# Seven-product calls of a second FFN: two sums of weight blocks move from the vector engine to accumulating transfers, and one product moves to the end

## The chip, the core and the metric

One core of a Trainium2 chip runs the whole kernel. The metric is the device time in microseconds of one execution. The kernel before was run three times: 1250.19, 1249.74 and 1250.16 us, median 1250.16 us.

Engines carry the profile's names: PE (TensorE, matrix products), PEld (its weight loads), DVE (VectorE), ACT (ScalarE), POOL (GpSimd) and SP (SyncE). SP only issues transfers; POOL issues the accumulating ones and otherwise does a little arithmetic. Each engine takes its instructions in order.

## What is computed

The reference is one decoder layer over 512 tokens of width 1024, followed by a normalisation. What matters here is its last feed-forward step:

```python
x = x + 0.5 * swiglu_ffn(rmsnorm(x, ffn2_norm), ffn2_w_in, ffn2_w_down)

def swiglu_ffn(x, w_in, w_down):
    a, b = jnp.split(x @ w_in, 2, axis=-1)
    return (jax.nn.silu(a) * b) @ w_down
```

`ffn2_w_in` is 1024 x 5632 (twice 2816 columns, for `a` and for `b`), `ffn2_w_down` is 2816 x 1024. All is fp32.

## The kernel before

**Products in three parts.** To keep fp32 accuracy, each operand is split into a rounded high part and a low rest. `split` (L118 to L126) makes `wh` from a weight tile on ACT (L124) and then `wl` as the difference on DVE (L125). The tags `wh` and `wl` have three buffers each. Every block then costs three matrix instructions: high x high, high x low rest of the activations, low rest x high.

**The seven-product calls.** The second FFN works on columns of `w_in` in steps of two 128-column tiles, `f` = 0, 2, ..., 20. The first three steps (0, 2, 4) are plain. The eight from `f` = 6 to `f` = 20 are done by `fast_in` (L1141 to L1209), a scheme with seven half-size products in place of eight; a call is named here by its `f` (call 6, call 8, ...). With the four blocks of the call's weights named a11 and a12 (columns of `a`, upper and lower half of the rows) and their counterparts in the `b` columns, a call does this:

- `s1` = upper plus lower half of the `b` columns: SP loads the one (L1150), POOL then issues an accumulating transfer from DRAM that adds the other (L1151).
- `ra` (tile `wraw`, two buffers, shared with the loads of `w_down`) holds a11 and a12.
- `s3` likewise from a load (L1154) and an accumulating transfer (L1155); `q22` is a plain load (L1157).
- `s2` = `s1` + a11 (DVE, L1184) and `s4` = `s2` + a12 (DVE, L1192), each in a buffer of its own. `s1`, `s3`, `q22`, `s2` and `s4` share the tag `wq` with five buffers.
- the products, in source order: `s1` x t1, a11 x b11, a12 x b21, `s2` x t2, `s4` x b22, `s3` x t3, `q22` x t4. A product is named by its activations: t1, b11, b21, t2, b22, t3, t4. In PE's rows t1h and t1l are the parts of t1, while b21 and b22 read the tiles uh and ul. Each product has 24 instructions of 128 x 256: 12 for the first of two output tiles (j = 0), 12 for the second.
- between them, copies and additions out of PSUM (ACT at L1186, L1189, L1195; DVE at L1199, L1201), and at the end tanh, two multiplications and the split into `gh` and `gl` (L1206 to L1209). t2, t3 and t4 go on accumulating in the same PSUM half, so t3 waits for the copy at L1195 and t4 for the addition at L1201.

**Around the calls.** The `f` go in groups of six, six, six and four. After the first call of a group `down2` (L1211) does the previous group's product with `w_down`, 144 (for the last group 96) instructions of 128 x 512. So calls 8, 10 and 12 stand back to back, then comes a `down2`, then 14, 16 and 18, another `down2`, call 20, and the last `down2` with the final normalisation.

**Order.** A scheduler sets the order of the instructions on each engine, and the pools decide which buffer a tile gets and so what a load waits for. Within a call's source order the scheduler may interleave products.

Of the kernel before, what the change touches and what calls it, by code (L numbers as in the profile page):

```python
# [15 lines left out]
ALU = mybir.AluOpType  # L16
# [68 lines left out]
def kernel(ctx, tc, x, mem, ffn1_norm, ffn1_w_in, ffn1_w_down, mix_norm, w_in, a_re, a_im, log_dt,  # L85
                             b_re, b_im, c_re, c_im, d_skip, w_glu, rel_table, w_up_attn, mem_norm, w_kv, w_up_mem,
                             w_out, ffn2_norm, ffn2_w_in, ffn2_w_down, final_norm, onehot, parity, out):
    nc = tc.nc
    V, S, G, TE = nc.vector, nc.scalar, nc.gpsimd, nc.tensor
    x, mem, out = x[0], mem[0], out[0]  # L90

    def sb_pool(name, side="left"):
        return tc.tile_pool(name=name, bufs=1, side=side, reuse_waits="tile")
# [13 lines left out]
    def load_chunk(w, k0, nk, c0, ncol):  # L107
        raw = wpool.tile([P, nk, ncol], F32, name="wraw", tag="wraw", bufs=2)
        nc.sync.dma_start(raw, w[k0 * P:(k0 + nk) * P, c0:c0 + ncol].rearrange("(k p) c -> p k c", p=P))
        return raw  # L110
# [9 lines left out]
    def split(raw, eng=V):  # L120
        _, nk, n = raw.shape
        h = wpool.tile([P, nk, n], F32R, name="wh", tag="wh", bufs=3)
        l = wpool.tile([P, nk, n], F32R, name="wl", tag="wl", bufs=3)
        S.activation(h, raw, AF.Copy)  # L124
        eng.tensor_tensor(l, raw, h.bitcast(F32), op=ALU.subtract)  # L125
        return h, l  # L126
# [15 lines left out]
    def split_plain(src, h, l, eng=V):  # L142
        S.activation(h, src, AF.Copy)  # L143
        eng.tensor_tensor(l, src, h.bitcast(F32), op=ALU.subtract)
# [26 lines left out]
    def ps_tile(tag, bufs=None):  # L171
        return ps["pool"].tile([P, T], F32, name="ps_" + tag, tag="ps_" + tag, bufs=ps["mm"] if tag == "mm" else bufs)
# [845 lines left out]
    with sb_pool("att") as ap:  # L1018
# [9 lines left out]
        for hp in range(2):  # L1028
            pacc = ps_tile("acc", 1)
            for r in range(4):  # L1030
# [12 lines left out]
                j = d % 2  # L1043
# [16 lines left out]
    op = wo_stack.enter_context(sb_pool("wo", "right"))  # L1060
# [34 lines left out]
    left, right = slice(0, HT), slice(HT, T)  # L1095
# [45 lines left out]
    def fast_in(w, f, pool, g):  # L1141

        def quarter(nm):
            return pool.tile([P, 4, 2 * P], F32, name=nm, tag="wq", bufs=5)

        def src(k0, c0):
            return w[0][k0 * P:(k0 + 4) * P, c0 + f * P:c0 + (f + 2) * P].rearrange("(k p) c -> p k c", p=P)

        s1 = quarter("s1")
        nc.sync.dma_start(s1, src(0, FF))  # L1150
        nc.gpsimd.dma_start(s1, src(4, FF), accum_op=ALU.add)  # L1151
        ra = load_chunk(w[0], 0, KD, f * P, 2 * P)
        s3 = quarter("s3")
        nc.sync.dma_start(s3, src(0, FF))  # L1154
        nc.gpsimd.dma_start(s3, src(0, 0), accum_op=ALU.add)  # L1155
        q22 = quarter("q22")
        nc.sync.dma_start(q22, src(4, FF))  # L1157
        a11, a12 = ra[:, :4, :], ra[:, 4:, :]
        px = [ps_tile("mm") for _ in range(2)]
        py = [ps_tile("mm") for _ in range(2)]  # L1160
        a = [pool.tile([P, T], F32, name="ff_a", tag="ff_a", bufs=3) for _ in range(2)]
        e5 = [pool.tile([P, HT], F32, name="ff_e", tag="ff_e", bufs=2) for _ in range(2)]

        def moving(n):
            if n in comb[0]:
                return [(comb[0][n][:, k], comb[1][n][:, k]) for k in range(4)]
            base, half = {"b21": (4, left), "b22": (4, right)}[n]
            return [(uh[base + k][:, half], ul[base + k][:, half]) for k in range(4)]

        def product(block, n, dst, half, start):  # L1170
            h, l = split(block)
            rhs = moving(n)
            for j in range(2):
                o, cols = dst[j][:, half], slice(j * P, (j + 1) * P)
                for k in range(4):
                    st = dict(start=start and k == 0, skip_group_check=True)
                    TE.matmul(o, h[:, k, cols], rhs[k][0], stop=False, **st)  # L1177
                    st["start"] = False
                    TE.matmul(o, h[:, k, cols], rhs[k][1], stop=False, **st)  # L1179
                    TE.matmul(o, l[:, k, cols], rhs[k][0], stop=k == 3, **st)  # L1180

        product(s1, "t1", py, right, True)
        s2 = quarter("s2")
        V.tensor_tensor(s2, s1, a11, op=ALU.add)  # L1184
        for j in range(2):
            S.activation(e5[j], py[j][:, right], AF.Copy)  # L1186
        product(a11, "b11", px, left, True)
        for j in range(2):
            S.activation(a[j][:, left], px[j][:, left], AF.Copy)  # L1189
        product(a12, "b21", py, left, False)  # L1190
        s4 = quarter("s4")
        V.tensor_tensor(s4, s2, a12, op=ALU.add)  # L1192
        product(s2, "t2", px, left, False)
        for j in range(2):
            S.activation(a[j][:, right], px[j][:, left], AF.Copy)  # L1195
        product(s4, "b22", py, right, False)
        product(s3, "t3", px, left, False)
        for j in range(2):
            V.tensor_tensor(a[j], a[j], py[j], op=ALU.add)  # L1199
        for j in range(2):  # L1200
            V.tensor_tensor(px[j][:, right], px[j][:, left], e5[j], op=ALU.add)  # L1201
        product(q22, "t4", px, left, False)

        for j in range(2):
            t = pool.tile([P, T], F32, name="ff_t", tag="ff_t", bufs=2)
            S.activation(t, a[j], AF.Tanh, scale=-0.5)  # L1206
            V.scalar_tensor_tensor(t, t, 1.0, a[j], op0=ALU.subtract, op1=ALU.mult)
            V.tensor_tensor(t, t, px[j], op=ALU.mult)
            split_plain(t, *g[f + j])  # L1209
# [79 lines left out]
    for f0, nf in groups:  # L1289
        for f in range(f0, f0 + nf, 2):  # L1290
            g.update(hidden(fp, f, 2))
            if f < 6:
                ffn_in(ffn2_w_in, f, fp, g, True, 3, steps2)
            else:
                fast_in(ffn2_w_in, f, fp, g)
                if f == 6:
                    natural_x2()
            if f == f0 and pend is not None:
                down2(*pend, False)
        pend = (f0, nf)  # L1300
# [34 lines left out]
```

## Time and profile before

The profiled execution took 1250.94 us; its span, from the first to the last instruction, is 1249.2 us. So 1.7 us lie around the span, and this execution is 0.8 us over the median of the runs.

| What | Value |
|---|---|
| Median of three runs | 1250.16 us |
| Profiled execution / its span | 1250.94 / 1249.2 us |
| Mean granted TensorE clock | 0.998 |
| Busy: PE / DVE / ACT / POOL | 1231.3 / 793.7 / 466.8 / 101.6 us |
| Seven-product calls, first and last rows of L1177 | 953.4 to 1222.7 us |

How to read it: the page gives busy time per engine and the chain of work that ended last. The timelines give single instructions as start, duration, engine, line, operation and tiles, with the idle time before it and what ended that in brackets. "DMA to landing" counts from the issue of a transfer to the arrival of its data.

### The profile page before, as it was taken

Reading aid. Unit: us, or ns where it says so; the run is one execution under the profiler, and the core shown is the slowest. Engines: PE = TensorE matmul, PEld = TensorE weight load, DVE = VectorE, ACT = ScalarE, POOL = GpSimd, SP = SyncE. Lnnn points to the kernel's source line nnn. Section 1 sums busy time; section 2 is a strip of 40 time slices with the busy share of each in tenths; the row PEclk is TensorE's granted clock in tenths of the full one; section 3 lists DMA queues with packets and bytes.
Section 4 is the critical chain, followed back from the end, with each engine's and each line's share of the span. In section 5 each row is a group of like instructions: output and inputs, shape, how many; then the busy total and the mean of one; then the engine's idle time right before and its main releaser. Section 6 shows DMA issues by size and latency. Waiting matters only on the chain.

```text
span 1249.2 us, 17053 instructions
## 1 busy us (share of the span) xinstructions
PE 1231.3 (99%) x6692; PEld 1046.2 (84%) x6692; DVE 793.7 (64%) x1514; ACT 466.8 (37%) x731; POOL 101.6 (8%) x83
## 2 busy tenths in 40 slices
PE   8999999999999999999999999999999999999997
PEld 6888888788888889998877788888789899899896
DVE  7999556875637666754536654554498557657664
ACT  4332232224325443224433544343345445345343
POOL 3000000000003023230000000002100001001002
PEclk9999999999999999999999999999999999999999
DMA  6233423764317755644118221335625457457411
GB/s 194 93 117 115 140 93 85 180 188 143 107 51 248 239 172 156 203 143 126 52 34 194 68 68 43 101 111 164 172 82 157 115 148 183 123 148 182 122 61 67
DMA packets 165767, 162.01 MB, mean 130 GB/s; under 512 B 28180, under 2 KB 149076, under 8 KB 165396
## 3 DMA queue, kind: packets, MB, share of 16 engines
q1 hardware_dynamic: 133488, 137.68, 35.3%
q0 software_dynamic: 8576, 8.65, 4.7%
q10 hardware_dynamic: 23624, 14.61, 4.0%
q8 instruction: 52, 0.85, 0.3%
q14 instruction: 27, 0.22, 0.1%
HBM read 145.94 MB, written 16.16 MB: 130 GB/s over the span
## 4 chain that ended last, share of the span: by engine, by line
PE 94%; DMA 2%; DVE 2%; ACT 1%; issue 0%; SPq 0%; ACTq 0%; DVEq 0%
PE ps_mm L133 20%; PE ps_mm L134 20%; PE ps_mm L135 20%; PE ps_mm L1179 4%; PE ps_mm L1180 4%; PE ps_mm L1177 4%; PE ps_mm L1235 3%; PE ps_mm L1237 3%; PE ps_mm L1236 3%; PE ps_acc L905 1%; PE ps_sc L898 1%; PE ps_sc L742 1%; DMA wraw<-in_ffn_w_in_dram 1%; DMA wraw<-in_xattn_w_kv_dram 1%; DVE wl L125 1%; PE ps_mm L833 1%
## 5 line engine op out<-in xcount | busy, mean ns | idle before, releaser
L124 ACT ACTIVATE wh<-wraw 128x1024 fp32r<-128x1024 f32 (+2 forms) x226 | 211.2, 938 | 468.4 <-PE ps_mm L134 321.2
L125 DVE TENSOR_TENSOR wl<-wraw,wh 128x1024 fp32r<-128x1024 f32 (+2 forms) x226 | 248.6, 1102 | 145.8 <-ACT wh L124 139.8
L133 PE MATMUL ps_mm<-uh,wh 128*128 128x512 f32 x736 | 288.9, 393 | 1.2 <-ACT wh L124 0.9
L135 PE MATMUL ps_mm<-uh,wl 128*128 128x512 f32 x736 | 287.9, 391 | 0.0
L134 PE MATMUL ps_mm<-ul,wh 128*128 128x512 f32 x736 | 287.6, 391 | 0.0
L133 PEld LDWEIGHTS ps_mm<-uh,wh 128*128 128x128 f32 x736 | 138.3, 188 | 30.1 <-issue 1.7
L135 PEld LDWEIGHTS ps_mm<-uh,wl 128*128 128x128 f32 x736 | 138.2, 188 | 28.7 <-issue 0.2
L134 PEld LDWEIGHTS ps_mm<-ul,wh 128*128 128x128 f32 x736 | 138.3, 188 | 28.5 <-issue 0.2
L217 POOL TENSOR_TENSOR sqacc<-sqacc,sqk 128x512 f32<-128x512 f32 x12 | 20.2, 1681 | 680.7 <-ACT sqk L216 680.6
L134 PE MATMUL ps_mm<-gl,wh 128*128 128x512 f32 x176 | 70.0, 398 | 0.0
L133 PE MATMUL ps_mm<-gh,wh 128*128 128x512 f32 x176 | 69.9, 399 | 0.0
L135 PE MATMUL ps_mm<-gh,wl 128*128 128x512 f32 x176 | 69.8, 398 | 0.0
L1236 PE MATMUL ps_mm<-wl,gh 128*128 128x512 f32 x176 | 69.4, 394 | 0.0
L1237 PE MATMUL ps_mm<-wh,gl 128*128 128x512 f32 x176 | 69.1, 394 | 0.0
L1235 PE MATMUL ps_mm<-wh,gh 128*128 128x512 f32 x176 | 67.6, 395 | 0.0
L125 DVE TENSOR_TENSOR wl<-s,wh 128x1024 fp32r<-128x1024 f32 x32 | 39.2, 1224 | 42.6 <-ACT wh L124 42.5
L124 ACT ACTIVATE wh<-s 128x1024 fp32r<-128x1024 f32 x32 | 33.9, 1061 | 61.4 <-PE ps_mm L1237 26.1
L143 ACT ACTIVATE gh<-ff_t 128x512 fp32r<-128x512 f32 x44 | 27.1, 627 | 52.3 <-DVE ff_t L315 33.3
L135 PEld LDWEIGHTS ps_mm<-gh,wl 128*128 128x128 f32 x176 | 33.0, 188 | 8.2 <-issue 0.2
L133 PEld LDWEIGHTS ps_mm<-gh,wh 128*128 128x128 f32 x176 | 33.0, 188 | 8.2 <-issue 0.2
L1237 PEld LDWEIGHTS ps_mm<-wh,gl 128*128 128x128 f32 x176 | 33.1, 188 | 7.7
L1236 PEld LDWEIGHTS ps_mm<-wl,gh 128*128 128x128 f32 x176 | 33.2, 188 | 7.5
(415 smaller groups left out, 2444.1 us busy)
## 6 DMA issues: line engine op xcount, KB each, us to landing
wraw<-in_ffn_w_in_dram SPq DMA_DIRECT2D x34, 1024.0 KB, 5.1
wraw<-in_w_in_dram SPq DMA_DIRECT2D x25, 1024.0 KB, 5.3
wraw<-in_ffn_w_down_dram SPq DMA_DIRECT2D x12, 768.0 KB, 4.6
s<-in_ffn_w_in_dram SPq DMA_DIRECT2D x16, 512.0 KB, 3.6
s<-in_ffn_w_in_dram POOLq DMA_DIRECT2D x16, 512.0 KB, 6.2
wraw<-in_ffn_w_down_dram SPq DMA_DIRECT2D x8, 1024.0 KB, 5.1
wraw<-in_ffn_w_down_dram SPq DMA_DIRECT2D x10, 512.0 KB, 3.5
wraw<-in_xattn_w_kv_dram SPq DMA_DIRECT2D x4, 1024.0 KB, 8.1
```

What stands on the lines that cost most here:

```text
L124: S.activation(h, raw, AF.Copy)
L125: eng.tensor_tensor(l, raw, h.bitcast(F32), op=ALU.subtract)
L133: TE.matmul(ps, h[:, k, :], rhs[k][0], start=first and k == 0, stop=False)
L134: TE.matmul(ps, h[:, k, :], rhs[k][1], start=False, stop=False)
L135: TE.matmul(ps, l[:, k, :], rhs[k][0], start=False, stop=last and k == n - 1)
L143: S.activation(h, src, AF.Copy)
L1177: TE.matmul(o, h[:, k, cols], rhs[k][0], stop=False, **st)
L1179: TE.matmul(o, h[:, k, cols], rhs[k][1], stop=False, **st)
L1180: TE.matmul(o, l[:, k, cols], rhs[k][0], stop=k == 3, **st)
L1235: TE.matmul(pd[r], gh[:, tok], h, start=st, stop=False)
L1236: TE.matmul(pd[r], gh[:, tok], l, start=False, stop=False)
L1237: TE.matmul(pd[r], gl[:, tok], h, start=False, stop=en)
```

## The change

The two DVE additions go. In their place POOL issues accumulating transfers from one place of SBUF to another: `s1` += a11 after the first product's split, and `s1` += a12 after the split for t2. The tiles `s2` and `s4` no longer exist; the fourth block sum's product, b22, stands last in source order, and the addition of `py` into `a` follows it.

```diff
         product(s1, "t1", py, right, True)
-        s2 = quarter("s2")
-        V.tensor_tensor(s2, s1, a11, op=ALU.add)
+        nc.gpsimd.dma_start(s1, a11, accum_op=ALU.add)
...
         product(a12, "b21", py, left, False)
-        s4 = quarter("s4")
-        V.tensor_tensor(s4, s2, a12, op=ALU.add)
-        product(s2, "t2", px, left, False)
+        product(s1, "t2", px, left, False)
+        nc.gpsimd.dma_start(s1, a12, accum_op=ALU.add)
         for j in range(2):
             S.activation(a[j][:, right], px[j][:, left], AF.Copy)
-        product(s4, "b22", py, right, False)
         product(s3, "t3", px, left, False)
-        for j in range(2):
-            V.tensor_tensor(a[j], a[j], py[j], op=ALU.add)
         for j in range(2):
             V.tensor_tensor(px[j][:, right], px[j][:, left], e5[j], op=ALU.add)
         product(q22, "t4", px, left, False)
+        product(s1, "b22", py, right, False)
+        for j in range(2):
+            V.tensor_tensor(a[j], a[j], py[j], op=ALU.add)
```

From here on acc1 is the transfer `s1` += a11 (L1183 of the changed kernel) and acc2 is `s1` += a12 (L1191). Lines from L1185 on are one or two lower in the changed kernel than before.

POOL's order from call 8 on. `s1_` and `s3_` are the sums of a call. Before, `s1_8914` belongs to call 8, `s1_9158` to call 10, `s1_9402` to call 12, `s1_9838` to call 14:

```order
L1151 DMA s1_8914<-in_ffn2_w_in_dram 128x4x256
L1155 DMA s3_8919<-in_ffn2_w_in_dram 128x4x256
L1151 DMA s1_9158<-in_ffn2_w_in_dram 128x4x256
L1155 DMA s3_9163<-in_ffn2_w_in_dram 128x4x256
L1151 DMA s1_9402<-in_ffn2_w_in_dram 128x4x256
L1155 DMA s3_9407<-in_ffn2_w_in_dram 128x4x256
```

In the changed kernel `s1_8912` is of call 8, `s1_9154` of call 10, `s1_9396` of call 12 and `s1_9830` of call 14; `wraw_` is the call's `ra`:

```order
L1183 DMA s1_8912<-wraw_8915 128x1024
L1191 DMA s1_8912<-wraw_8915 128x1024
L1151 DMA s1_9396<-in_ffn2_w_in_dram 128x4x256
L1183 DMA s1_9154<-wraw_9157 128x1024
L1155 DMA s3_9401<-in_ffn2_w_in_dram 128x4x256
L1191 DMA s1_9154<-wraw_9157 128x1024
L1151 DMA s1_9830<-in_ffn2_w_in_dram 128x4x256
L1183 DMA s1_9396<-wraw_9399 128x1024
```

Four transfers a call pass through POOL instead of two, and the next-but-one sum of a later call (`s1_9396` of call 12) stands ahead of call 10's acc1.

SP's order at the same place, before (`wraw_9405` is call 12's):

```order
L109 DMA wraw_9161<-in_ffn2_w_in_dram 128x8x256
L1150 DMA s1_9158<-in_ffn2_w_in_dram 128x4x256
L109 DMA wraw_9405<-in_ffn2_w_in_dram 128x8x256
L1154 DMA s3_9163<-in_ffn2_w_in_dram 128x4x256
L1157 DMA q22_9166<-in_ffn2_w_in_dram 128x4x256
L1150 DMA s1_9402<-in_ffn2_w_in_dram 128x4x256
```

And in the changed kernel (`wraw_9399` is call 12's, `q22_9162` call 10's):

```order
L109 DMA wraw_9157<-in_ffn2_w_in_dram 128x8x256
L1157 DMA q22_9162<-in_ffn2_w_in_dram 128x4x256
L109 DMA wraw_9399<-in_ffn2_w_in_dram 128x8x256
L1150 DMA s1_9396<-in_ffn2_w_in_dram 128x4x256
L1154 DMA s3_9401<-in_ffn2_w_in_dram 128x4x256
L1157 DMA q22_9404<-in_ffn2_w_in_dram 128x4x256
L109 DMA wraw_9638<-in_ffn2_w_down_dram 128x4x512
```

Call 12's `wraw_9399` takes call 8's buffer, which acc1 and acc2 of call 8 now read, so its load waits until both have landed; the load of `s1_9396` has moved right behind it on SP.

PE's order in call 10 of the changed kernel, at the end of the first half of t3 (output tile `ps_mm_9164`); the rows with `uh4` and `ul4` are the first of b22, whose `wh_9350` is made from `s1` after acc2:

```order
L1180 MATMUL ps_mm_9164<-t3h_7861,wl_9293 128x256
L1177 MATMUL ps_mm_9166<-uh4_101,wh_9350 128x256
L1179 MATMUL ps_mm_9166<-ul4_109,wh_9350 128x256
L1177 MATMUL ps_mm_9167<-uh4_101,wh_9350 128x256
L1179 MATMUL ps_mm_9167<-ul4_109,wh_9350 128x256
L1177 MATMUL ps_mm_9165<-t3h_7861,wh_9292 128x256
```

Although b22 is last in the source, the scheduler has put four of its 24 rows between the halves of t3; after the other half of t3 follow 16 more, then all of t4, then the last four and t1 of the next call. Before, all 24 rows of b22 stood between t2 and t3.

## Prediction

> **What bounds the kernel now.** I read the page first: busy time and the chain that ended last.
>
> ```profile
> PE 1231.3 (99%) x6692; PEld 1046.2 (84%) x6692; DVE 793.7 (64%) x1514; ACT 466.8 (37%) x731; POOL 101.6 (8%) x83
> PE 94%; DMA 2%; DVE 2%; ACT 1%; issue 0%; SPq 0%; ACTq 0%; DVEq 0%
> ```
>
> An average says little about one stage, so next the windows around the calls 8 to 12, 14 to 18, the last call and the end (columns: window, length, then busy time of PE, PEld, DVE, ACT, POOL, clock, DMA share, GB/s).
>
> ```profile
> 1010.00:1074.00 64.00, 64.00 (x514) 63.00 (x514) 45.10 (x53) 33.35 (x49) 7.70 (x6) 1.00 0.69 165
> 1104.00:1168.00 64.00, 64.00 (x515) 63.04 (x514) 45.07 (x53) 33.35 (x49) 7.72 (x6) 1.00 0.71 166
> 1198.00:1230.00 32.00, 32.00 (x220) 29.73 (x219) 17.50 (x23) 15.35 (x24) 0.00 (x0) 1.00 0.11 34
> 1230.00:1250.00 20.00, 11.09 (x48) 8.66 (x46) 10.90 (x33) 8.38 (x24) 8.64 (x6) 0.88 0.28 105
> ```
>
> PE is busy for every one of 64, 64 and 32 us: nothing that feeds it is late. DVE has 19 us free in each 64. So DVE time that goes is not on the path, and there is no PE wait here that the change could remove. The change can only leave PE as full as it is, or open gaps. The question is whether the sums still arrive in time.
>
> **What is removed.** One addition a call at L1184 and one at L1192.
>
> ```profile
> L1184 DVE TENSOR_TENSOR s<-s,wraw x8: 1218/1222/1226, 940.5 to 1184.2; 128x1024 f32<-128x1024 f32 x8
> L1192 DVE TENSOR_TENSOR s<-s,wraw x8: 1217/1220/1227, 943.0 to 1185.5; 128x1024 f32<-128x1024 f32 x8
> ```
>
> 16 x 1.22 = 19.5 us of DVE, all hidden by the full PE: worth 0. PE's instructions are the same in number and shape: 0.
>
> **The rhythm it must keep.** Timeline rows of call 8 (start, duration): PE's first two rows of t1 and the first of b11; then the first of t2, and a split beside it, ACT's part and DVE's part.
>
> ```profile
> 1010.74 0.28 PE L1177 MATMUL ps_mm<-t1h,wh 128*128 128x256 f32 x1
> 1010.86 0.29 PE L1179 MATMUL ps_mm<-t1l,wh 128*128 128x256 f32 x1
> 1013.62 0.28 PE L1177 MATMUL ps_mm<-b11h,wh 128*128 128x256 f32 x1
> 1019.37 0.28 PE L1177 MATMUL ps_mm<-t2h,wh 128*128 128x256 f32 x1
> 1019.46 1.06 ACT L124 ACTIVATE wh<-s 128x1024 fp32r<-128x1024 f32 x1 [1.54 <-PE ps_mm L1179]
> 1020.55 1.23 DVE L125 TENSOR_TENSOR wl<-s,wh 128x1024 fp32r<-128x1024 f32 x1 [1.65 <-ACT wh L124]
> ```
>
> A matmul takes 0.12 us, a product 24 of them, 2.88 us. A split starts 0.09 us after the product that frees its buffer has ended (three buffers: the product three splits earlier), and is done 1.1 us (high part) and 2.3 us (low part) after its start. Seven products are 20.16 us a call.
>
> **What is added: two accumulating transfers a call, 512 KB each.** The trace shows none inside SBUF. The nearest rows are the accumulating ones from DRAM (durations of the POOL instruction in ns; landing after issue in us), then plain loads of 512 KB and 1 MB, and the two queues:
>
> ```profile
> L1151 POOL DMA_DIRECT2D s<-in_ffn_w_in_dram x8: 1273/1282/1356, 895.0 to 1146.2; - x8
> DMA to landing us min/median/max: 5.9/7.8/9.1
> L1155 POOL DMA_DIRECT2D s<-in_ffn_w_in_dram x8: 1282/1282/1301, 897.7 to 1157.7; - x8
> DMA to landing us min/median/max: 5.7/6.0/9.0
> s<-in_ffn_w_in_dram SPq DMA_DIRECT2D x16, 512.0 KB, 3.6
> wraw<-in_ffn_w_down_dram SPq DMA_DIRECT2D x10, 512.0 KB, 3.5
> wraw<-in_ffn_w_in_dram SPq DMA_DIRECT2D x34, 1024.0 KB, 5.1
> q1 hardware_dynamic: 133488, 137.68, 35.3%
> q0 software_dynamic: 8576, 8.65, 4.7%
> ```
>
> Per packet of about 1 KB (share x 16 engines x 1249.2 us / packets), q0 takes 0.110 us and q1 0.053: accumulating costs twice. 512 packets over 16 engines are then 3.5 us of the 6.0, which leaves 2.5 us fixed. Bounds for the transfer inside SBUF: 2.5 + 1.7 = 4.2 us at the plain price, and 7.8 us, the median that L1151 has among other loads. I take 5.6: nearest is the quiet accumulate, 6.0, less 0.4, since these rows are 4 KB long and a load with rows twice as long is 0.1 us quicker (3.5 against 3.6), twice over, at twice the price. So 3.1 us of data.
>
> The Trainium skill's page "DMA: Bandwidth & Descriptors" (section "Anatomy of one DMA — SWDGE (gpsimd) path") puts a transfer on this path at 2.0 us plus its bytes at 436 GB/s; by it, as an estimate, 512 KB would land in 3.2 us, and by that the added term would be 0 (first rival). The trace does not bear that out for accumulating transfers from DRAM, where 5.7 us is the least; for one inside SBUF no run here shows it yet.
>
> The chain that is new: split for t1, acc1, split for t2, acc2, split for b22, and only then t1 of the next call on ACT. Before, `s2` and `s4` needed only the loads and could be added early.
>
> **Calls 8 and 14 (and 20), after a `down2`.** The split for t1 was early: ACT's row at 1003.97 is 6.8 us ahead of PE's 1010.74.
>
> ```profile
> 1003.97 1.06 ACT L124 ACTIVATE wh<-s 128x1024 fp32r<-128x1024 f32 x1 [8.70 <-PE ps_mm L1237]
> ```
>
> With T the start of t1: low part done at T-4.5, acc1 lands by T+1.2. The split for t2 starts when t1 frees its buffer, T+3.0, and with DVE's row behind another is done at about T+5.4. acc2 issues at T+5.5 and lands at T+11.1; the split for b22 starts with the end of t2, T+11.6, and ends at T+12.7. PE reaches b22's first rows after four and a half products, T+12.96. Cost 0, with 0.3 us to spare. Below, zero is this moment in call 8: acc2 has landed at -1.9.
>
> **Calls 10, 12, 16 and 18: POOL's queue.** PE now goes on (0.48 + 1.44 + 1.92 + 2.88 + 0.48) and starts call 10's t1 at 7.2, would start t2 at 15.84 and reach b22 at 20.16. The split for t1 waits for t3's buffer: start 2.0, done 4.3. acc1 could issue then. But POOL has call 12's L1151 ahead of it. That waits for the load of `s1_9396`, which on SP stands behind `wraw_9399`, which waits for call 8's acc2. POOL waits for such loads already:
>
> ```profile
> 1052.46 1.28 POOL L1151 DMA_DIRECT2D s<-in_ffn_w_in_dram  x1 [7.27 <-DMA s<-in_ffn_w_in_dram]
> ```
>
> Today nothing urgent stands behind such a wait. Now: issue -1.8; 1 MB lands after 5.1 us, the 512 KB behind it 1.7 us of data later, at 5.0. L1151 holds POOL from 5.1 to 6.4 and lands at 11.1. acc1 issues at 6.4 and lands at 12.0, but its data follow on the same queue: 11.1 + 3.1 = 14.2. The split for t2 runs 14.3 to 15.4 on ACT and to 16.7 on DVE. PE's third row of t2 wants the low part at 16.1: **0.6 us** lost. t2 ends at 19.3.
>
> acc2 issues at 16.8 and would land at 22.4; the load of q22 for call 12, free once t3 is split, overlaps its last part (0 to 1.7 us, the data of 512 KB; I take half, 0.8): 23.2. Split on ACT, PE goes on at 24.4. Wanted at 19.3 + 1.44 = 20.7: **3.7 us** lost. Nothing later on PE can pass, since its four b22 rows stand ahead of the second half of t3 and of t4.
>
> Sum 4.3 us a call; the same pattern stands ahead of acc1 in calls 12 (the load of call 14's `s1` behind a `w_down` load that waits for acc2 of call 10), 16 and 18. 4 x 4.3 = 17.2 us. With a transfer of 5.1 us the same steps give 2.3 a call, 9 us; with 6.0 they give 5.4, 22 us.
>
> **The end.** The last `w_down` load takes call 20's `ra` buffer, now held until acc2 lands, T+11.1. ACT's split of it stands ahead of the rest of ACT's work, and on DVE its first two parts stand ahead of the addition that lets t4's second half start. Rows of before: ACT's four, DVE's four, the addition; then PE's last row of a `down2` and T, 0.23 us later.
>
> ```profile
> 1206.20 2.19 ACT L143 ACTIVATE wh<-wraw 128x512 fp32r<-128x512 f32 x4 [0.54 <-DMA wraw<-in_ffn_w_down_dram]
> 1206.86 2.50 DVE L144 TENSOR_TENSOR wl<-wraw,wh 128x512 fp32r<-128x512 f32 x4 [0.21 <-ACT wh L143]
> 1216.72 0.42 DVE L1201 TENSOR_TENSOR ps_mm<-ps_mm,ff_e 128x256 f32<-128x256 f32 x1
> 1198.26 0.39 PE L1237 MATMUL ps_mm<-wh,gl 128*128 128x512 f32 x1
> 1198.49 0.28 PE L1177 MATMUL ps_mm<-t1h,wh 128*128 128x256 f32 x1
> ```
>
> Load issued T+11.2, landed T+16.3; two parts split by T+18.2; addition done T+18.7. PE wants it at T+18.5 (12.96 + 3.84 + 1.44 + 0.24). Cost 0.2 us, up to 2 if the load meets others; I take 0.5. That a's addition now follows the last product is hidden: its second half needs some 4 us (addition, tanh, two multiplications, split), and 25 rows of `down2` that need only calls before 20, at 0.23 us, stand on PE ahead of its use: 5.7 us.
>
> **Sum.** 17.2 + 0.5 = 17.7, say 18 us. The profiled execution would go from 1250.9 to 1268.9; it lies 0.8 over the median, so 1268.
>
> **The rivals.**
>
> *The transfer is quick and all stays hidden.* Inside SBUF no DRAM is read; at 4.2 us or less acc1 lands at 11.4, t2's split is done at 13.8, and acc2 lands at 18.1, before t2 frees the buffer at 18.7. No gap: 1250, or 1252 with the end. It decides at about 4.5 us. (The page's 3.2 us would be this case.) For it: plain 512 KB lands in 3.6. Against: no accumulate in the trace lands under 5.7. Chance 0.11, of which 0.09 within the bound below and 0.02 faster, by a better packed end (at most the 8.9 us that PE is idle in the last window).
>
> *The transfer is slow, and every call stalls.* At 7.8 us, what L1151 has at the median, acc2 of calls 8, 14 and 20 comes 1.5 us late, and in the four others, by the steps above with 5.3 us of data, t2 loses 3.5 and b22 5.7: 4 x 9.2 + 3 x 1.5 = 41, so 1291. For it: DMA share 0.7 in these windows, and 16 more transfers of over 3 us data. Against: SP's loads mostly come between. Chance 0.17.
>
> *My forecast*, stalls in four calls for a transfer between 4.6 and 6.6 us, 1255 to 1279: 0.72.
>
> **How the numbers follow.** A measurement tells about 0.2% from no change, 2.5 us. Leaving out the hidden case and the upper part of the slow one gives 1254 to 1284. Faster 0.02, same 0.09, slower 0.89.
>
> **What would show it.** In the profile after: PE idle in the windows of calls 10, 12, 16, 18 with "ACT wh L124" before a b22 row, 3 to 4 us each, less before t2; none of weight in calls 8 and 14. POOL idle before L1151 by its own load, and acc1 directly behind. L1183 and L1191 landing near 5.6 us, acc1 of those calls later than that by its queue. DVE down by 19.5 us. I am wrong if PE stays full there, if calls 8 and 14 stall as much as 10, or if POOL reaches acc1 without delay.

## The result, and the profile after

Five runs of the changed kernel have a median of 1270.11 us (1268.50 to 1270.98), five of the kernel before 1250.19 us (1249.74 to 1252.88). The ratio, estimated from all the runs, is 1.0152, with a 95% interval from 1.0140 to 1.0163; the two medians alone give 1.0159. The forecast was 1268.0 us in a range from 1254 to 1284, with slower at 0.89.

The page of the changed kernel: busy time of the engines, then the queue of POOL's transfers with its packets, MB and share. The span is 1268.1 us.

```profile
PE 1237.5 (98%) x6692; PEld 1050.6 (83%) x6692; DVE 775.4 (61%) x1498; ACT 464.9 (37%) x731; POOL 115.3 (9%) x99
q0 software_dynamic: 10880, 17.04, 8.3%
```

DVE is down by 18.3 us, near to the 19.5 of the 16 removed additions, and the time has gone up. The windows around the calls 8 to 12 and 14 to 18 of the changed kernel show why; the columns are those of the windows in the prediction.

```profile
1014.00:1084.00 70.00, 63.23 (x514) 62.05 (x513) 40.02 (x48) 32.39 (x49) 12.29 (x11) 1.00 0.77 177
1116.00:1186.00 70.00, 65.11 (x515) 63.90 (x514) 40.40 (x49) 33.10 (x49) 9.71 (x9) 0.98 0.70 160
```

PE, full before, is idle for 6.8 and 4.9 of 70 us. The groups of instructions, from 930 us to the end, say where: one group has all of the idle time of the calls.

```profile
L1177 PE MATMUL ps_mm<-uh,wh 128*128 128x256 f32 x128 | 37.5, 295 | 13.6 <-ACT wh L124 7.3 <-ACT ff_e L1185 6.3
```

The tile `uh` names b21 and b22. Half of the waiting is for a split by ACT (the four calls' b22), half for ACT's copy `ff_e` (b21, in these four calls and in call 6).

The first product's first row marks a call's start. These rows of the changed kernel start the calls 6, 8, 14 and 20.

```profile
954.17 0.28 PE L1177 MATMUL ps_mm<-t1h,wh 128*128 128x256 f32 x1
1015.02 0.28 PE L1177 MATMUL ps_mm<-t1h,wh 128*128 128x256 f32 x1
1116.67 0.28 PE L1177 MATMUL ps_mm<-t1h,wh 128*128 128x256 f32 x1
1217.96 0.28 PE L1177 MATMUL ps_mm<-t1h,wh 128*128 128x256 f32 x1
```

And of the kernel before, calls 6 and 14 (8 and 20 stand in the prediction, at 1010.74 and 1198.49):

```profile
953.65 0.28 PE L1177 MATMUL ps_mm<-t1h,wh 128*128 128x256 f32 x1
1104.62 0.28 PE L1177 MATMUL ps_mm<-t1h,wh 128*128 128x256 f32 x1
```

From call 8 to 14 it was 93.88 us and is 101.65; from 14 to 20 it was 93.87 and is 101.29. That is 7.77 + 7.42 = 15.2 us in the calls 10, 12, 16 and 18. From call 6 to 8 it was 57.09 and is 60.85: 3.8 us that the prediction does not have. The start adds 0.5, the stretch behind t1 of call 20 loses 0.6 (50.71 before, 50.14 now). Together 18.9 us, the difference of the spans.

Now call 10 by the row. Its zero, the moment when PE reaches b22 in call 8, is 1027.96 here. First SP and POOL, t1 of this call, then ACT's split for t2 and the copy behind it, b21's second half, acc2, the split for b22, and b22:

```profile
1026.07 0.37 SPq L1150 DMA_DIRECT2D s<-in_ffn_w_in_dram  x1
1033.47 1.30 POOL L1151 DMA_DIRECT2D s<-in_ffn_w_in_dram  x1 [12.03 <-DVE ff_a L1200]
1034.23 1.46 POOL L1183 DMA_DIRECT2D s<-wraw  x1
1035.14 0.28 PE L1177 MATMUL ps_mm<-t1h,wh 128*128 128x256 f32 x1
1042.18 1.06 ACT L124 ACTIVATE wh<-s 128x1024 fp32r<-128x1024 f32 x1 [4.11 <-DMA s<-wraw]
1043.14 0.37 ACT L1185 ACTIVATE ff_e<-ps_mm 128x256 f32<-128x256 f32 x1
1043.56 0.39 PE L1177 MATMUL ps_mm<-uh,wh 128*128 128x256 f32 x1 [1.06 <-ACT ff_e L1185]
1044.79 0.88 POOL L1191 DMA_DIRECT2D s<-wraw  x1 [7.77 <-DVE wl L125]
1050.30 1.06 ACT L124 ACTIVATE wh<-s 128x1024 fp32r<-128x1024 f32 x1 [3.19 <-DMA s<-wraw]
1051.41 0.39 PE L1177 MATMUL ps_mm<-uh,wh 128*128 128x256 f32 x1 [1.83 <-ACT wh L124]
```

POOL sat idle for 12 us ahead of L1151, the accumulating transfer for call 12. Its bracket names a DVE instruction (L1200, the addition of `py` into `a`, which was L1199 before) that ended at 1032.87 and makes nothing that L1151 reads. What L1151 adds to is call 12's load: L1150 issued it only at 1026.07, and it landed at 1032.92. In all four calls L1151 starts 0.55 or 0.56 us behind the landing of its load, while the bracket names different DVE instructions. Acc1 of call 10 issues right behind, 0.8 us later, and ACT stands idle for 4.11 us until it has landed. The split then holds up the copy queued behind it, and the copy holds up b21: PE loses its first 1.06 us there, before it has come to t2 at all. Acc2 follows from t2's split, and the split for b22 from acc2: 1.83 us more.

### The profile page after: what moved, and what is told of

Its sections match the earlier page's. It is cut to its first block, busy times and chain, and to the rows that moved or that the text cites. A ratio compares the mean times of both kernels' runs of the same rounds, so it can differ in the third digit from the quotient of the medians.

```text
span 1268.1 us, 17068 instructions
## 1 busy us (share of the span) xinstructions
PE 1237.5 (98%) x6692; PEld 1050.6 (83%) x6692; DVE 775.4 (61%) x1498; ACT 464.9 (37%) x731; POOL 115.3 (9%) x99
## 5 line engine op out<-in xcount | busy, mean ns | idle before, releaser
L1177 PE MATMUL ps_mm<-uh,wh 128*128 128x256 f32 x128 | 37.5, 295 | 13.6 <-ACT wh L124 7.3
```

## The experiments

All experiments compute the same sums. The experiments ran on three chips, on which the kernel before has medians of 1251.58, 1250.65 and 1250.03 us. The columns behind the ratio show the profiled execution of each: the time from t1 of call 6 to t1 of call 8, from there to call 14 and on to call 20, by the rows of `t1h`; PE's waits of over 0.3 us behind t1 of call 6; and how many stretches there are, from t1 of call 6 on and ahead of the last stage, in which the granted clock is 0.50 (of these more below). The ratios compare with runs of the kernel before on the same chip. Of e_pool_order the slowest of nine executions was profiled, 1258.6 us; its t1 of call 6 starts 3.4 us later than in the changed kernel, behind a wait of 1.8 us at 397 us and a further stretch at clock 0.50 behind that, in a stage far ahead of the calls.

| Kernel | Median, us | Ratio (95%) | 6 to 8 | 8 to 14 | 14 to 20 | Waits, us | Clock 0.50 |
|---|---|---|---|---|---|---|---|
| before | 1250.19 | 1 | 57.09 | 93.88 | 93.87 | 0 | 0 |
| changed | 1270.11 | 1.0152 (1.0140 to 1.0163) | 60.85 | 101.65 | 101.29 | 13.6 | 2 |
| e_vec_inplace | 1253.97 | 1.0021 (1.0011 to 1.0030) | 59.25 | 93.85 | 93.84 | 1.7 | 0 |
| e_pool_order | 1255.07 | 1.0032 (1.0022 to 1.0042) | 60.65 | 94.44 | 93.85 | 1.7 | 1 |
| e_b22_last | 1271.84 | 1.0170 (1.0154 to 1.0185) | 59.35 | 102.87 | 101.57 | 14.4 | 2 |
| e_both | 1257.77 | 1.0057 (1.0042 to 1.0072) | 60.78 | 95.37 | 94.28 | 4.3 | 1 |
| e_call6_before | 1266.28 | 1.0123 (1.0108 to 1.0138) | 57.08 | 103.13 | 100.74 | 9.7 | 2, one of 6.8 us |
| e_pool_call6 | 1250.85 | 0.9995 (0.9984 to 1.0005) | 57.09 | 93.86 | 93.88 | 0 | 0 |
| e_acc1_only | 1271.72 | 1.0166 (1.0150 to 1.0181) | 60.82 | 101.34 | 102.60 | 12.0 | 5 |
| e_acc2_only | 1254.34 | 1.0027 (1.0017 to 1.0036) | 60.56 | 93.84 | 93.85 | 2.1 | 0 |
| e_copy_first | 1271.65 | 1.0172 (1.0155 to 1.0189) | 59.00 | 104.48 | 105.05 | 15.6 | 3 |
| e_pool_copy | 1257.50 | 1.0063 (1.0045 to 1.0080) | 58.46 | 96.65 | 96.61 | 4.9 | 0 |

**The transfers or the order of the products?** The sums stay in place, but DVE makes them:

```diff
-        nc.gpsimd.dma_start(s1, a11, accum_op=ALU.add)
+        V.tensor_tensor(s1, s1, a11, op=ALU.add)
...
-        nc.gpsimd.dma_start(s1, a12, accum_op=ALU.add)
+        V.tensor_tensor(s1, s1, a12, op=ALU.add)
```

> Both sums are made in place by additions on DVE (s1 += a11, s1 += a12, some 1.2 us each) instead of by transfers; the products keep the changed kernel's order, with b22 between the halves of t3. Theory (the transfers' time in series is the loss): the sums are ready 3 to 5 us sooner each, the stalls ahead of b21 and b22 in calls 10, 12, 16 and 18 go, 1250 to 1254 us, of which up to 3.8 us may be call 6's own loss. Rival (the order of the products, or holding s1 and ra longer, is the loss): 1265 to 1270 us.

1253.97 us, and the stretches from call 8 to 14 and 14 to 20 are those of the kernel before within 0.03 us. PE's order from call 8 to 20 is that of the changed kernel. So neither b22's place on PE nor holding `s1` and `ra` until DVE has made the second sum costs anything in these calls; the transfers do. (Here both come free sooner than with a transfer; that the longer hold costs nothing either is shown by e_pool_call6 below.) Call 6 still loses 2.2 us, with no transfer inside SBUF in it.

**POOL's queue.** The next call's L1151 may issue only behind acc1:

```diff
+        with ExitStack() as behind:
+            if "acc1" in last:
+                behind.enter_context(tc.issue_after(last["acc1"]))
+            nc.gpsimd.dma_start(s1, src(4, FF), accum_op=ALU.add)
-        nc.gpsimd.dma_start(s1, src(4, FF), accum_op=ALU.add)
...
-        nc.gpsimd.dma_start(s1, a11, accum_op=ALU.add)
+        last["acc1"] = nc.gpsimd.dma_start(s1, a11, accum_op=ALU.add).ins
```

> As changed, but the next call's L1151 may issue on POOL only behind this call's acc1, so acc1 no longer stands behind a wait for a load. Theory (POOL's queue makes acc1 late, and the lateness goes on to acc2): acc1 issues some 2 to 4 us sooner in calls 10, 12, 16 and 18, the stalls ahead of b21 go and those ahead of b22 are under 0.7 us each; 1254 to 1258 us, with call 6's 3.8 us left. Rival (two transfers of 5.4 us in series are too long by themselves, the queue does not matter): b22 still waits 1.8 us a call, 1266 to 1271 us. Third: the delayed L1151 makes the next call's t1 late, new waits ahead of t1: 1260 us or more, with the stalls at another place.

1255.07 us: 15 us of the loss are gone with both transfers still there. From call 8 to 20 PE, ACT, DVE and SP have the same instructions in the same order as in the changed kernel; only POOL's order differs. Call 10 in the timeline of this kernel (acc1 is L1188 here and the next sum's transfer L1156): POOL's two rows, t1 of call 10, ACT's split for t2.

```profile
1035.76 0.86 POOL L1188 DMA_DIRECT2D s<-wraw  x1 [11.10 <-DVE wl L125]
1036.31 1.64 POOL L1156 DMA_DIRECT2D s<-in_ffn_w_in_dram  x1
1038.34 0.28 PE L1182 MATMUL ps_mm<-t1h,wh 128*128 128x256 f32 x1
1041.53 1.06 ACT L124 ACTIVATE wh<-s 128x1024 fp32r<-128x1024 f32 x1 [0.27 <-DMA s<-wraw]
```

Acc1 issues 2.6 us ahead of t1, and its split starts 3.2 us behind t1. In the changed kernel t1 of call 10 starts at 1035.14, so acc1 issued 0.9 us ahead of it and the split started 7.0 us behind it. Of the 3.9 us that the split is earlier, 1.7 are acc1's issue; the other 2.2 are its transfer, which no longer has L1151's data ahead of it on the queue (5.8 us from issue to split instead of 8.0). Nothing else comes late by L1151's new place. PE's waits from 900 us on, all of them:

```profile
PE ps_mm L1182 <- ACT ff_e L1190: 1.4, 1, 1.4
PE ps_mm L135 <- DVE wl L125: 0.5, 1, 0.5
PE ps_mm L1182 <- ACT wh L124: 0.3, 1, 0.3
PE ps_mm L1185 <- DVE wl L125: 0.2, 1, 0.2
```

The first is call 6's. The rival, that two transfers in series are too long by themselves, is refuted.

**Each sum alone.** In one kernel only a12's sum goes back to DVE in place, in the other only a11's (the two lines of the first diff, one each).

> Only the first sum is a transfer; the second (s1 += a12) is made in place on DVE. Theory (acc1's delay of 2 us behind L1151 stays, but the second sum follows in 1.2 us instead of 5.4): waits ahead of b21 or t2 may stay at up to 1.3 us in four calls, none ahead of b22; 1252 to 1260 us. Rival (the loss is acc1's alone): 1265 us or more.

> Only the second sum is a transfer; the first (s1 += a11) is made in place on DVE. Theory: t2's sum is ready early, acc2 issues when t2's split is done, some 2 us sooner than in the changed kernel, and lands before b22 wants it or just behind; 1250 to 1256 us. Rival (the loss is acc2's alone, since one transfer late in a call is enough): 1258 us or more, with the waits ahead of b22.

The second came as expected: 1254.34 us, nothing lost from call 8 on. The first did not: 1271.72 us, and the rival is right that acc1 alone is enough. The timeline of that kernel at call 10, POOL's three rows and t1:

```profile
1032.58 1.30 POOL L1151 DMA_DIRECT2D s<-in_ffn_w_in_dram  x1 [19.79 <-DMA s<-in_ffn_w_in_dram]
1035.33 1.28 POOL L1155 DMA_DIRECT2D s<-in_ffn_w_in_dram  x1 [1.46 <-DMA s<-in_ffn_w_in_dram]
1036.08 1.45 POOL L1183 DMA_DIRECT2D s<-wraw  x1
1036.18 0.28 PE L1177 MATMUL ps_mm<-t1h,wh 128*128 128x256 f32 x1
```

Here acc1 stands behind two waits for loads, L1151's and L1155's, and issues only with t1 of its own call. The edit made the one suspected wait longer, so this kernel does not show acc1's share in the changed one; it shows that a late acc1 needs no acc2 to cost this much. The waits are fewer than in the changed kernel (12.0 against 13.6 us), the time is not, and the windows behind two of the waits say why:

```profile
1045.50:1048.50 3.00, 3.00 (x14) 3.00 (x15) 3.00 (x4) 2.31 (x5) 0.00 (x0) 0.50 0.00 0
1148.00:1151.00 3.00, 3.00 (x16) 3.00 (x16) 3.00 (x5) 1.66 (x3) 0.00 (x0) 0.50 0.17 14
```

The granted clock is 0.50. This kernel has five such stretches of some 3.4 us, the changed one two.

**b22 where the source has it.**

```diff
-        product(q22, "t4", px, left, False)
-        product(s1, "b22", py, right, False)
+        with tc.issue_after(product(q22, "t4", px, left, False)):
+            product(s1, "b22", py, right, False)
```

> As changed, but all 24 rows of b22 stand behind t4 on PE, as the source has them, instead of four between the halves of t3. Theory (acc2 is 2 us late for the place that the scheduler gave b22): the four waits of 1.8 us ahead of b22 go and those ahead of b21 stay; 1260 to 1263 us. Rival (b22's lateness is passed on to the next call's t1, since the split for t1 stands behind the split for b22 on ACT): the waits move to t1, 1268 to 1272 us.

1271.84 us; the theory fell. The rival had the size right and the place wrong: not t1 of the next call waits, but t3, 4.9 us in the four calls; and the waits at b21 grow from 4.4 to 6.7 us. Call 10 of this kernel, ACT's split for b22, the copy behind it (L1194, out of the tile that t3 adds to), and the second half of t3:

```profile
1047.72 1.06 ACT L124 ACTIVATE wh<-s 128x1024 fp32r<-128x1024 f32 x1 [2.46 <-DMA s<-wraw]
1048.68 0.36 ACT L1194 ACTIVATE ff_a<-ps_mm 128x256 f32<-128x256 f32 x1
1049.10 0.39 PE L1177 MATMUL ps_mm<-t3h,wh 128*128 128x256 f32 x1 [1.54 <-ACT ff_a L1194]
```

b22 itself has moved away from the late sum, but ACT's queue has not: the split still stands ahead of a copy that PE needs soon. It is the same pattern as at b21. With L1151 behind acc1 as well:

> As changed, with L1151 behind acc1 on POOL and all of b22 behind t4. Theory (queue and place of b22 are all there is to the loss in the four calls): no waits of weight from call 8 on, 1250 to 1256 us, what is left being call 6's. Rival (the longer chain makes t1 of the next call late): 1262 us or more, with waits ahead of t1.

1257.77 us, between the ranges of the theory and of the rival. The queue's part of the gain is there, b22's place adds nothing to it and costs 2.7 us: call 12 still waits 0.98 us at t3, by the same copy, and the last call 1.46 us at t4.

**The copy ahead of the splits.** If ACT's queue is what passes the lateness on, the copies of e5 can be put ahead:

```diff
-            S.activation(e5[j], py[j][:, right], AF.Copy)
+            copied = S.activation(e5[j], py[j][:, right], AF.Copy).ins
...
-        product(a12, "b21", py, left, False)
-        product(s1, "t2", px, left, False)
+        with tc.issue_after(copied):
+            product(a12, "b21", py, left, False)
+            product(s1, "t2", px, left, False)
```

> As changed, but on ACT both copies of e5 (L1185) stand ahead of the splits for b21 and t2, so that b21's second half no longer waits for a copy queued behind the late split. Theory (the late sum costs, whichever row it meets first; acc2's landing sets PE's time at b22): the waits ahead of b21 go in calls 10, 12, 16 and 18, but t2 and b22 wait in their place, together within 1 us of the changed kernel's for each call; call 6 gains up to 3 us; 1264 to 1270 us. Rival (the place of the copy on ACT is the loss): the waits ahead of b21 go and nothing comes in their place, 1256 to 1262 us.

1271.65 us, a little above the theory's range. PE's waits from 900 us on, all of them:

```profile
PE ps_mm L1177 <- ACT wh L124: 12.3, 7, 2.5
PE ps_mm L1177 <- ACT ff_a L1188: 2.8, 3, 1.6
PE ps_mm L1180 <- DVE wl L125: 0.5, 1, 0.5
```

None is for the copy L1185 any more, and nothing is won: b22 waits 2.3 to 2.5 us where it waited 1.8, and t2 waits 0.5 to 1.6 in three calls. So the late sum costs wherever PE meets it. From call 8 to 20 this kernel even loses 21.8 us, 6.6 more than the changed one: 2.1 in the calls 8 and 14, where the later split for b21 is the edit's own new wait (0.8 us each, and what a wait costs beside itself), about 3.0 by two more stretches at half the clock, 0.9 by longer waits; some 0.6 us are not accounted for. Call 6, of which the section below tells, gains 1.9 us by the edit.

**Call 6.** It is put back as it was before, sums and order, the other calls stay changed; and the same with L1151 behind acc1.

```diff
+        if f == 6:
+            s2 = quarter("s2")
+            V.tensor_tensor(s2, s1, a11, op=ALU.add)
+        else:
+            nc.gpsimd.dma_start(s1, a11, accum_op=ALU.add)
-        nc.gpsimd.dma_start(s1, a11, accum_op=ALU.add)
```

(and so for `s4`, the place of b22 and that of the addition of `py`).

> Call 6 as in the kernel before (s2 and s4 on DVE, the products in the old order), the other calls as changed. Theory (call 6 has a loss of its own, 3.8 us, by the order of ACT's and DVE's work there): 1265 to 1267 us, the waits in calls 10, 12, 16 and 18 as they were. Rival (call 6's loss is not due to its own sums): 1269 to 1271 us.

> Call 6 as before and, in the others, L1151 of the next call behind acc1 on POOL. Theory (queue on POOL plus call 6 make up the loss): 1250 to 1254 us. Rival (latency in series, not the queue): 1264 to 1268 us.

1266.28 and 1250.85 us, both as the theory has it. (In the first the waits of the four calls are not quite as they were: 9.7 us instead of 11.6, but with 10.2 us at half the clock behind them instead of 3.4.) The two edits account for the whole loss: 15.0 us by POOL's order, 3.8 by call 6, and with both the ratio to the kernel before is 0.9995 (0.9984 to 1.0005). The windows of this last kernel around the calls 8 to 12, 14 to 18 and 6:

```profile
1009.00:1079.00 70.00, 70.00 (x547) 68.20 (x546) 45.03 (x54) 36.14 (x53) 10.91 (x10) 1.00 0.90 213
1103.00:1173.00 70.00, 70.00 (x547) 68.19 (x546) 44.92 (x54) 35.51 (x53) 9.62 (x9) 1.00 0.81 190
930.00:1009.00 79.00, 79.00 (x442) 68.92 (x441) 53.23 (x79) 35.79 (x58) 6.05 (x5) 1.00 0.52 145
```

PE is full, with 14 accumulating transfers inside SBUF and a DMA share up to 0.90. DVE has 14.5 us less to do than in the kernel before (779.2 against 793.7), and the time does not move: DVE's time was worth nothing, as the prediction said.

What call 6 loses, and why. Rows of the changed kernel in call 6: ACT's split for b21, the first copy of e5, and PE's b21.

```profile
960.17 1.04 ACT L124 ACTIVATE wh<-wraw 128x1024 fp32r<-128x1024 f32 x1
961.64 0.36 ACT L1185 ACTIVATE ff_e<-ps_mm 128x256 f32<-128x256 f32 x1
962.05 0.58 PE L1177 MATMUL ps_mm<-uh,wh 128*128 128x256 f32 x1 [1.96 <-ACT ff_e L1185]
```

And ACT's split for b21 and the same copy in the kernel before:

```profile
954.08 1.05 ACT L124 ACTIVATE wh<-wraw 128x1024 fp32r<-128x1024 f32 x1
955.66 0.38 ACT L1186 ACTIVATE ff_e<-ps_mm 128x256 f32<-128x256 f32 x1
```

Both come 6 us later now, while t1 of the call starts only 0.5 us later. The scheduler has ordered ACT's and DVE's work of this stage anew: the high parts of t3 and t4 (ACT rows at 957.98 and 958.83) now stand ahead of the split, where before they came behind the copy (955.94 and 957.91). The copy stands behind the late split. One more kernel has L1151 behind acc1 and the copies ahead of the splits, in all calls:

> As changed, with L1151 of the next call behind acc1 on POOL and, on ACT, the copies of e5 ahead of the splits for b21 and t2; all sums are transfers, call 6's too. Theory (what is left in 1255 us with L1151 behind acc1 is call 6, where a copy of e5 stands behind the split for b21 on ACT): 1251 to 1253 us. Rival (call 6 loses by the late parts of u and of the sums ahead of it, not by the copy): 1254 to 1256 us.

1257.50 us, outside of both ranges: call 6 gains 2.2 us against e_pool_order (58.46 instead of 60.65), but the splits for b21, now behind the copies, make b21 wait 0.6 to 0.8 us in each of the calls 8 to 18. So the copy's place is most of call 6's loss, with the stretch at half the clock that its wait brings. Of the 1.4 us that remain, 0.9 are waits at b21 for its own split. What led the scheduler to the other order there stays open; that it needs no transfer inside SBUF is shown by e_vec_inplace, which loses 2.2 us there with the two sums on DVE.

## Why the prediction was right, step by step

**Calls 8, 14 and 20 cost 0: right.** PE reaches b22 of call 8 at 1027.96, 12.94 us behind t1 (predicted 12.96), without a wait, and calls 14 and 20 have none either.

**The transfer, 5.6 us: right, a little high.** The two transfers of the changed kernel by line:

```profile
L1183 POOL DMA_DIRECT2D s<-wraw x8: 856/1170/1455, 951.6 to 1213.8; - x8
DMA to landing us min/median/max: 4.5/6.2/8.1
L1191 POOL DMA_DIRECT2D s<-wraw x8: 856/871/891, 965.7 to 1223.5; - x8
DMA to landing us min/median/max: 4.5/5.3/5.4
```

4.5 us at the least, 5.3 at the median where nothing of POOL's own is ahead (acc2), up to 8.1 where L1151 is (acc1). The bounds were 4.2 and 7.8; the longest is 0.3 us above them. By the Trainium skill's page "DMA: Bandwidth & Descriptors" (section "Anatomy of one DMA — SWDGE (gpsimd) path") the estimate was 3.2 us; the trace does not agree, since 4.5 us is the least inside SBUF too.

**POOL's queue in calls 10, 12, 16 and 18: right, to 0.5 us.** Behind the zero, L1151 issues at +5.5 (predicted 5.1), acc1 at +6.3 (6.4), the split for t2 at +14.2 (14.3), acc2 at +16.8 (16.8). This is call 10; in the calls 12, 16 and 18 acc1 also issues 0.8 us behind L1151, after POOL was idle for 12.2, 11.4 and 12.3 us. The experiment with L1151 behind acc1 shows that this is the cause.

**t2's low part loses 0.6 us: the step that failed.** t2 loses nothing; b21 loses 1.06, 2.04, 0.70 and 0.56 us ahead of it. The prediction followed the late split to the product that it feeds, not to what stands behind it on ACT: the second copy of e5, which b21's second half needs. e_copy_first, where the copy goes first, has the waits at t2 and b22 instead, and gains nothing.

**b22 loses 3.7 us: the place is right, the size twice too much.** It loses 1.8 us in each of the four calls. Its split starts at +22.3 (predicted 23.2), 5.5 us behind acc2's issue instead of the 6.4 that were counted with the load of q22 beside it. And PE has come to b22 at +21.6 instead of 20.7, having waited at b21 already.

**Sum of the four calls: 17.2 us predicted, 15.2 measured.** The waits there are 11.6 us (13.6 less call 6's 1.96). One stretch at half the clock adds 1.5. The rest, some 0.25 us for each of eight waits, is that the next matmul could have started 0.16 us before the end of the last one by the records (0.28 us long, every 0.12), and that the first one behind a wait takes 0.1 us more: 11.6 + 1.5 + 2.0 = 15.1. So the waits alone are a third below the forecast, and two costs that the prediction did not have, half the clock and the restart behind a wait, make up 3.5 us. The prediction's side sums, 9 us for a transfer of 5.1 us and 22 for one of 6.0, do not follow from its steps either: with its 0.8 us for the load of q22 held, they give some 3.3 and 5.0 us a call, 13 and 20 us.

**What was not in the sum.** Call 6, taken at nothing, loses 3.8 us (1.96 of waiting, 1.5 of half clock, 0.25 as above). The end, taken at 0.5, gains 0.6. That 1268 came so near to 1270.1 is in part luck: two terms too high by 2.0 and 1.1 us, one missing by 3.8, 0.5 at the start; and inside the 15.2, waits shorter than forecast and costs that were left out partly cancel.

**The rivals.** "Quick, all hidden" was to decide at 4.5 us: that is the least the trace shows, and in the four calls it is 5.3 and more. "Slow, every call stalls" needed acc2 of calls 8, 14 and 20 to land more than 0.3 us later than forecast; b22 did not wait for it there. What the prediction did not have among its rivals: the same two transfers on a queue in another order cost 0.5 us (e_pool_order) or nothing (e_pool_call6) from call 8 on.

## What to carry to other kernels

Before an instruction goes to a queue that runs in order, look at what already waits there: a prefetch that may sit on its load for 12 us is harmless until something urgent is queued behind it, and moving the prefetch behind it gave back 15 of the 20 us lost. Follow a late result not only to the instruction that reads it but to all that stands behind that one on its engine; here the first to stall was a product that did not use the late sum. Work taken off an engine with time to spare need not give anything back: DVE lost 14.5 us of it in e_pool_call6, and the time stayed.

## What the runs showed of the hardware

PE's clock falls to half behind some waits, and that costs nearly as much as the wait itself. The windows of the changed kernel behind a wait of 1.82 us in call 16 and at the wait of 1.96 us in call 6:

```profile
1153.20:1156.50 3.30, 3.30 (x17) 3.30 (x17) 1.42 (x3) 0.60 (x1) 0.00 (x0) 0.50 0.96 357
962.00:965.50 3.50, 3.45 (x16) 3.45 (x17) 3.50 (x5) 2.65 (x6) 0.00 (x0) 0.51 0.19 70
```

And two rows in a row from the first of them:

```profile
1153.53 0.41 PE L1179 MATMUL ps_mm<-t3l,wh 128*128 128x256 f32 x1
1153.74 0.42 PE L1180 MATMUL ps_mm<-t3h,wl 128*128 128x256 f32 x1
```

Matmuls start every 0.21 us instead of every 0.12, for about 3.4 us: 3.4 x (1 - 0.12 / 0.21) = 1.5 us lost. In e_acc1_only all five waits of 1.75 to 3.67 us are followed by such a stretch, in e_pool_order one of 1.40 us; in the changed kernel one of 2.04 us is not, and none of under 1 us by itself is in any run. The Trainium skill's page "TensorE: Matmul & The Clock Gate" (section "Part 1: The HAM clock gate (the "warmup" mystery)") tells of a window of about 3.4 us that runs freely, of half speed after an idle one and full speed after a busy one. The length agrees with the stretches here. That the window runs freely agrees too: in every run with more than one stretch they start whole multiples of 3.413 us apart, by the trace's record of the clock at 962.05 and 1153.20 in the changed kernel (56 of them) and at 963.56, 1045.48, 1069.38, 1147.88 and 1171.78 in e_acc1_only (24, 7, 23 and 7). So where a wait falls on this grid matters. That a whole window of idle is needed does not agree, since 1.4 us were enough. How much is needed stays open: on this grid a window with 1.82 us of idle is followed by half the clock in call 16 of the changed kernel, and one with the same 1.82 us in call 12 is not. POOL's issue of an accumulating transfer took 0.86 us inside SBUF against 1.27 to 1.36 from DRAM (L1151 before), and 1.46 where it overlapped with another.
